# Stick-breaking attention: at most one scan piece between the transposes and the lower half, and y split one point after it is summed

## The chip, the core and the metric

The kernel runs on one core of a Trainium2 chip. The metric is the device time of one execution in microseconds. TensorE is written PE, VectorE DVE, ScalarE ACT, GpSimd POOL and SyncE, which only issues DMAs here, SP.

## What is computed

A decoder layer on 1024 positions of 1024 features in float32: half a SwiGLU feed-forward, two token mixers side by side (forgetting attention and stick-breaking attention, 8 heads of 64 each), a second half feed-forward, and a gated input embedding. The part that the change is in is the attention:

```python
def stick_breaking_attention(q, k, v):
    ...
        z = jnp.einsum('bqhd,bkhd->bhqk', qi, k).astype(jnp.float32) * scale
        mask = kpos[None, :] < pi[:, None]
        log_beta = jax.nn.log_sigmoid(z)
        log_1m = jnp.where(mask, jax.nn.log_sigmoid(-z), 0.0)
        after = lax.cumsum(log_1m, axis=3, reverse=True) - log_1m
        a = jnp.where(mask, jnp.exp(log_beta + after), 0.0)
        return jnp.einsum('bhqk,bkhd->bqhd', a.astype(v.dtype), v)
```

Forgetting attention is a causal softmax with an added bias; both end in the same product with v.

## The kernel before, in words

**Two halves.** A float32 factor is split into a higher half, rounded to the matmul's format, and a lower half, the rest. The higher half is a copy on ACT, the lower one a subtraction on DVE, and a product is the sum of two or three matmuls on these halves.

**Heads, steps and points.** `attention()` goes through 16 heads, of which the first 8 are forgetting attention ("fox") and the last 8 stick-breaking. A head has four steps c = 0 to 3. `scores` makes the two rows of 128 queries of a step (rows 2c and 2c+1): matmuls L1163 and L1164, then for stick-breaking the two sigmoids on ACT, G (L1171, buffers GF and RN in turn) and T (L1172). `apply` uses these rows two steps later. For each pair of key blocks (`kpair`, from c down to 0) `turn_and_scan` transposes the rows of T on PE into a bank of PSUM (L1222; there are two banks for it), copies the higher half out on ACT (L1224, tile PT), and subtracts the lower half out on DVE (`low`, L1230). `values` multiplies both halves with v (L1248) into the one bank `av`; the result is copied to the tile Y by ACT (L1274) and its other half added by DVE (L1277, `add`). In the first pair of a step the tile is 384 wide, in the others 512.

**Scans.** In stick-breaking the product over the later keys is a scan on DVE (L1126), in pieces of 256 keys of one row, and POOL then multiplies T by it (L1195). A piece is one scan, or two where it holds the diagonal (the masked 128 and the rest). Pieces wait in the list `pend`, and `pop()` takes one from it, or two when more than five wait; `pop(upto)` takes all up to a place in the order.

**Late work.** `late` holds what is done at the next `flush()`, of which there is one in each turn and one ahead of each row: the sum `add`, and behind it, when two heads and two steps of a Y tile are complete (`hh == 1 and c % 2`), y's division into halves: an ACT copy (L1283), a DVE subtraction (L1284) and two DMAs on SP (L1288, L1289) that write both halves to memory. The branch product reads them back (L1504) from head 13 on.

**Order.** PE's order in attention is the order of the code. For the last 8 heads ACT's copies L1224 and L1283 and DVE's instructions L1126, L1230, L1277 and L1284 keep the order of the code too (`order`); for the first 8 a list scheduler places them. In between, PE works on matmuls that fill up the time (L907, L915: projections of later heads; L1510: the branch product). POOL's L139 makes lower halves of weights from copies of ACT (L129).

Of the kernel before, what the change touches and what calls it, by code (L numbers as in the profile page):

```python
# [11 lines left out]
F32R = mybir.dt.float32r  # L12
# [6 lines left out]
P = 128  # L19
# [17 lines left out]
def tile_hybrid_decoder_layer(  # L37
# [6 lines left out]
    nc = tc.nc  # L44
# [7 lines left out]
    def nm(s):  # L52
        uid[0] += 1
        return f"{s}_{uid[0]}"

    def slot(tag, shape, dt=F32):
        pad = -shape[-1] % 16
        t = sb.tile([*shape[:-1], shape[-1] + pad], dt, tag=tag, bufs=BUFS[tag], name=nm(tag))
        return t[:, :, :shape[-1]] if pad else t
# [6 lines left out]
    def bank(tag):  # L66
        return pp.tile([P, 512], F32, tag=tag, bufs=PSUM[tag], name=nm("ps"))
# [12 lines left out]
    def pe(ins):  # L80
        order("pe", ins)

    def order(key, ins):
        prev = last.get(key)
        if prev is not None and not manual[0]:
            tc.add_manual_dep(ins.ins, prev.ins.name, NOSYNC, reason="order")
        last[key] = ins

    def f(ap):
        return ap.bitcast(F32)  # L90
# [72 lines left out]
    yd = dp.tile([8, 2, P, S], F32, name="y_pairs")  # L163
# [961 lines left out]
    def scan(*args):  # L1125
        order("dve", nc.vector.tensor_tensor_scan(*args))  # L1126

    def pop(upto=None):

        n = 1 + (len(pend) > 5)  # L1130
        while pend and (n if upto is None else pend[0][:2] <= upto):
            pend.pop(0)[2]()
            n -= 1

    pend, late = [], []

    def flush():
        while late:
            late.pop(0)()

    def scores(step, fill):
        step["pr"] = []
# [57 lines left out]
        for i in (2 * step["c"], 2 * step["c"] + 1):  # L1200
            pop((step["id"] - 2, 0))
            pop()
            flush()
            row(i)
            yield

    def apply(step, fill):
        c = step["c"]
        v2 = step["v"]["v"]
        hd = step["head"] % 4  # L1210
        av = bank("av")
        pts = {}

        def transposes(kpair):
            width = 512 if kpair < c else 384
            ps = bank("pt")
            for kb in (2 * kpair, 2 * kpair + 1):
                for j in range(2):
                    if kb == 2 * c + 1 and j == 0:
                        continue  # L1220
                    col = (kb % 2) * 256 + (j * P if kb < 2 * c + 1 else 0)
                    pe(nc.tensor.transpose(ps[:, col:col + P], step["pr"][j][:, kb * P:(kb + 1) * P], identf[:]))  # L1222
            pt = slot("PT", [P, 2, 512], F32R)
            high = nc.scalar.copy(pt[:, 0, :width], ps[:, :width])  # L1224
            if not step["fox"]:
                order("act", high)
            pts[kpair] = pt

            def low():
                ins = nc.vector.tensor_sub(pt[:, 1, :width], ps[:, :width], f(pt[:, 0, :width]))  # L1230
                if not step["fox"]:
                    order("dve", ins)
            return low

        def values(kpair):
            pt = pts[kpair]
            mm = []
            for kb in (2 * kpair, 2 * kpair + 1):
                for b in range(2):
                    c0 = (kb % 2) * 256  # L1240
                    if kb < 2 * c + 1:
                        mm.append((av[:, 0:256], v2[:, kb, hd, :], pt[:, b, c0:c0 + 256]))
                    else:
                        mm.append((av[:, P:256], v2[:, kb, hd, :], pt[:, b, c0:c0 + P]))
            if kpair == c:
                mm = [mm[0], mm[2], mm[3], mm[1]]
            for i, (o, lh, r) in enumerate(mm):
                pe(nc.tensor.matmul(o, lh, r, start=(kpair == c and i == 0), stop=(kpair == 0 and i == 3)))  # L1248

        def turn_and_scan(kpair):  # L1250
            low = transposes(kpair)
            pop()
            pop((step["id"], 2 - kpair))
            low()
            flush()
            fill()

        pop((step["id"], 1 - c))
        turn_and_scan(c)
        yield  # L1260
        for kpair in range(c - 1, -1, -1):
            turn_and_scan(kpair)
            if kpair + 2 <= c:
                values(kpair + 2)
            yield
        if c:
            values(1)
        fill()
        fill()
        values(0)  # L1270
        Y = step["y"]
        hh = step["head"] % 2
        ys = Y["t"][hh * HD:(hh + 1) * HD, c * 256:(c + 1) * 256]
        nc.scalar.copy(ys, av[HD:P, :256])  # L1274

        def add():
            ins = nc.vector.tensor_add(ys, av[0:HD, :256], ys)  # L1277
            if not step["fox"]:
                order("dve", ins)
            if hh == 1 and c % 2 and not step["last"]:  # L1280
                cs = slice(c // 2 * 512, c // 2 * 512 + 512)
                hi = slot("PT", [P, 512], F32R)
                a = nc.scalar.copy(hi[:], Y["t"][:, cs])  # L1283
                b = nc.vector.tensor_sub(Y["t"][:, cs].bitcast(F32R), Y["t"][:, cs], f(hi[:]))  # L1284
                if not step["fox"]:
                    order("act", a)
                    order("dve", b)
                nc.sync.dma_start(yd[Y["idx"], 0][:, cs], f(hi[:]))  # L1288
                nc.sync.dma_start(yd[Y["idx"], 1][:, cs], Y["t"][:, cs])  # L1289
        late.append(add)  # L1290

    FOX_PAIRS = [2, 3, 0, 1]
# [80 lines left out]
    def attention():  # L1373
# [109 lines left out]
        for step in prev:  # L1483
            run(apply(step, lambda: run(islice(rest, 6))))
        flush()
        run(rest)
        yt = ys[7]["t"]
# [340 lines left out]
```

## Time and profile before

| | |
|---|---|
| time, median of 3 runs | 2240.51 us (2239.74 to 2241.10) |
| the profiled execution: its own time, its span | 2238.65 us, 2236.9 us |
| PE busy | 2213.2 us, 99% of the span |
| DVE busy | 1515.7 us, 68% |
| ACT busy, POOL busy | 1004.8 us and 823.8 us |
| PE clock granted | 0.999 |
| transposes of attention, L1222 | from 849.9 us to 1372.1 us of the span |
| scans of stick-breaking, L1126 | from 1108.9 us to 1368.1 us |
| y's division, L1284 | 14 times, from 907.6 us to 1314.9 us |

In the rows a line stands for one group of instructions. In a timeline row the columns are start and duration in us, engine, line, operation, output and inputs, shapes and count; in brackets stands the idle time of the engine ahead of it and what ended that. In a row of waits stand who waited, for whom, the sum in us, how often, and the longest.

### The profile page before, as it was taken

Reading aid. Unit: us, or ns where it says so; the run is one execution under the profiler, and the core shown is the slowest. Engines: PE = TensorE matmul, PEld = TensorE weight load, DVE = VectorE, ACT = ScalarE, POOL = GpSimd, SP = SyncE. Lnnn points to the kernel's source line nnn. Section 1 sums busy time; section 2 is a strip of 40 time slices with the busy share of each in tenths; the row PEclk is TensorE's granted clock in tenths of the full one; section 3 lists DMA queues with packets and bytes.
Section 4 is the critical chain, followed back from the end, with each engine's and each line's share of the span. In section 5 each row is a group of like instructions: output and inputs, shape, how many; then the busy total and the mean of one; then the engine's idle time right before and its main releaser. Section 6 shows DMA issues by size and latency. Waiting matters only on the chain.

```text
span 2236.9 us, 30553 instructions
## 1 busy us (share of the span) xinstructions
PE 2213.2 (99%) x11226; PEld 1879.6 (84%) x11226; DVE 1515.7 (68%) x2365; ACT 1004.8 (45%) x1802; POOL 823.8 (37%) x793
## 2 busy tenths in 40 slices
PE   9999999999999999999999999999999999999998
PEld 7888888888888899999898888888888888888887
DVE  8855555598888324666678885789655455778897
ACT  6433333433455435555566663245333333333454
POOL 2444435200021336556556664520535344200111
PEclk9999999999999999999999999999999999999999
DMA  3332323394323334333324466741423232665336
GB/s 133 104 127 85 127 81 132 117 344 174 113 95 106 125 107 127 86 104 86 85 53 97 116 203 208 262 151 57 141 81 132 80 132 78 219 236 179 118 104 179
DMA packets 195607, 295.41 MB, mean 132 GB/s; under 512 B 28665, under 2 KB 108793, under 8 KB 195458
## 3 DMA queue, kind: packets, MB, share of 16 engines
q1 hardware_dynamic: 194448, 290.32, 39.2%
q0 software_dynamic: 1008, 3.15, 0.7%
q8 instruction: 88, 1.44, 0.3%
q14 instruction: 61, 0.50, 0.1%
q10 hardware_dynamic: 2, 0.00, 0.0%
HBM read 193.52 MB, written 83.13 MB: 124 GB/s over the span
## 4 chain that ended last, share of the span: by engine, by line
PE 88%; DVE 7%; ACT 2%; issue 1%; DMA 1%; POOL 0%; SPq 0%; DVEq 0%; ACTq 0%; POOLq 0%
PE ps L622 39%; PE ps L509 22%; PE ps L907 8%; PE ps L915 5%; PE ps L1510 4%; PE ps L1248 3%; PE ps L563 2%; PE ps L1222 2%; PE ps L1164 1%; PE ps L1163 1%; PE ps L1069 1%; DVE PT L1230 1%; DVE RN L1126 1%; DVE GF L1126 1%; DMA WH<-out_dram 1%
## 5 line engine op out<-in xcount | busy, mean ns | idle before, releaser
L509 PE MATMUL ps<-H,H 128*128 128x512 f32 x2184 | 497.3, 389 | 0.0
L509 PEld LDWEIGHTS ps<-H,H 128*128 128x128 f32 x2184 | 409.5, 188 | 84.9
L622 PE MATMUL ps<-H,WL 128*128 128x512 f32 x1164 | 275.0, 389 | 0.0
L622 PEld LDWEIGHTS ps<-H,WL 128*128 128x128 f32 x1164 | 218.5, 188 | 45.3
L185 POOL TENSOR_TENSOR PT<-PT,PT 128x512 f32<-128x512 f32 x27 | 34.9, 1294 | 403.8 <-ACT PT L182 402.9
L622 PE MATMUL ps<-H,Q 128*128 128x512 f32 x612 | 145.5, 389 | 0.0
L517 DVE SCALAR_TENSOR_TENSOR X<-ps,X 128x512 f32<-128x512 f32 x168 | 110.0, 683 | 47.5 <-PE ps L509 47.3
L622 PE MATMUL ps<-X,WL 128*128 128x512 f32 (+1 forms) x588 | 139.1, 386 | 2.6 <-ACT KH L1789 2.6
L622 PEld LDWEIGHTS ps<-H,Q 128*128 128x128 f32 x612 | 114.9, 188 | 23.8
L622 PE MATMUL ps<-H,PT 128*128 128x512 f32 x540 | 129.1, 390 | 1.6 <-ACT PT L105 0.9
L622 PEld LDWEIGHTS ps<-X,WL 128*128 128x128 f32 x588 | 109.2, 188 | 24.9 <-ACT KH L1789 2.8
L139 POOL TENSOR_TENSOR WL<-RAW,WH 128x512 fp32r<-128x512 f32 (+1 forms) x84 | 98.4, 1193 | 67.5 <-ACT WH L129 43.2
L622 PEld LDWEIGHTS ps<-H,PT 128*128 128x128 f32 x540 | 101.1, 188 | 23.4 <-ACT PT L105 1.3
L1230 DVE TENSOR_TENSOR PT<-ps,PT 128x512 fp32r<-128x512 f32 (+1 forms) x160 | 99.8, 626 | 29.6 <-ACT PT L1224 28.9
L907 PE MATMUL ps<-WH,H 128*128 128x256 f32 x768 | 116.1, 287 | 0.8 <-ACT RN L972 0.8
L915 PE MATMUL ps<-H,WH 128*128 128x512 f32 x384 | 115.0, 406 | 0.0
L1248 PE MATMUL ps<-PT,X 128*128 128x256 f32 (+1 forms) x640 | 102.3, 286 | 6.4 <-DVE PT L1230 5.4
L1224 ACT CAST PT<-ps 128x512 fp32r<-128x512 f32 (+1 forms) x160 | 87.1, 548 | 42.6 <-PE ps L1222 41.5
L1248 PEld LDWEIGHTS ps<-PT,X 128*128 128x128 f32 x640 | 90.2, 190 | 16.7 <-DVE PT L1230 10.2
L907 PEld LDWEIGHTS ps<-WH,H 128*128 128x128 f32 x768 | 101.4, 190 | 2.6 <-ACT RN L972 1.2
L412 POOL TENSOR_TENSOR PT<-GF,RN 128x512 f32<-128x512 f32 x20 | 33.6, 1682 | 185.3 <-DVE GF L815 185.3
L1176 POOL TENSOR_TENSOR T<-T,l 128x128 f32<-128x128 f32 (+3 forms) x64 | 73.2, 1147 | 71.8 <-DVE l L1175 69.7
(457 smaller groups left out, 4793.2 us busy)
## 6 DMA issues: line engine op xcount, KB each, us to landing
hidden<-PT SPq DMA_DIRECT2D x40, 512.0 KB, 3.1
WH<-in_ffn_w_gate_dram SPq DMA_DIRECT2D x38, 512.0 KB, 5.5
Q<-hidden SPq DMA_DIRECT2D x24, 512.0 KB, 5.6
hidden<-RN SPq DMA_DIRECT2D x22, 512.0 KB, 2.6
KH<-in_ffn_w_up_dram SPq DMA_DIRECT2D x20, 512.0 KB, 6.2
KL<-in_ffn_w_up_dram SPq DMA_DIRECT2D x20, 512.0 KB, 6.9
T<-in_ffn_w_down_dram SPq DMA_DIRECT2D x20, 512.0 KB, 6.2
GF<-hidden SPq DMA_DIRECT2D x14, 512.0 KB, 6.9
```

What stands on the lines that cost most here:

```text
L139: ins = eng_lo.tensor_sub(lo[part], raw[part], f(hi[part]))
L509: pe(nc.tensor.matmul(groups[g][t][:], wt[:, b, k, t * P:(t + 1) * P], act[:, a, k, :], start=(fresh and n == 0), stop=(i in (6, 1, 4) and ...
L517: nc.vector.scalar_tensor_tensor(xs, groups[g][t][:], scale, xs, ALU.mult, ALU.add)
L563: pe(nc.tensor.matmul(ps[:], hl[:, a, k, :], right(rb, b, k), start=(i == 0), stop=(i == 23)))
L622: pe(nc.tensor.matmul(ps[:, cols], hl[:, a, k, :], right(B[m], b, k)[:, cols], start=(first and i == 0), stop=(final and i == 11), skip_gr ...
L907: pe(nc.tensor.matmul(ps[:, :n], hT[t // 4](a, k)[:, (t % 4) * P:(t % 4 + 1) * P], w[k // 4][b][:, k % 4, :n], start=(i == 0), stop=(i == ...
L915: pe(nc.tensor.matmul(ps[:], w[a][:, k, :], hT[half](b, k), start=(i == 0), stop=(i == 23)))
L1176: nc.gpsimd.tensor_mul(T[:, :n], T[:, :n], l[:].broadcast_to([P, n]))
L1224: high = nc.scalar.copy(pt[:, 0, :width], ps[:, :width])
L1230: ins = nc.vector.tensor_sub(pt[:, 1, :width], ps[:, :width], f(pt[:, 0, :width]))
L1248: pe(nc.tensor.matmul(o, lh, r, start=(kpair == c and i == 0), stop=(kpair == 0 and i == 3)))
L1510: pe(nc.tensor.matmul(ps[:], w[a][:, k, :], yT[g][b][:, k, half * 512:half * 512 + 512], start=(i == 0), stop=(i == 11)))
```

## The change

`turn_and_scan` takes one piece from `pend` between the transposes and `low`; the second piece, if more than five were waiting, and the pieces that `pop(upto)` asks for come behind `low`. `flush` calls only what was in `late` when it began, and `add` no longer divides y itself but puts that into `late`, so that it comes at the next point.

```diff
-    def pop(upto=None):
+    def pop(upto=None, n=None):
 
-        n = 1 + (len(pend) > 5)
+        n = n or 1 + (len(pend) > 5)
...
     def flush():
-        while late:
-            late.pop(0)()
+        for call in [late.pop(0) for _ in range(len(late))]:
+            call()
...
         def turn_and_scan(kpair):
             low = transposes(kpair)
-            pop()
+            more = len(pend) > 5
+            pop(n=1)
+            low()
+            if more:
+                pop(n=1)
             pop((step["id"], 2 - kpair))
-            low()
             flush()
             fill()
...
             if hh == 1 and c % 2 and not step["last"]:
-                cs = slice(c // 2 * 512, c // 2 * 512 + 512)
-                hi = slot("PT", [P, 512], F32R)
-                a = nc.scalar.copy(hi[:], Y["t"][:, cs])
-                b = nc.vector.tensor_sub(Y["t"][:, cs].bitcast(F32R), Y["t"][:, cs], f(hi[:]))
...
+                late.append(parts)
+
+        def parts():
+
+            cs = slice(c // 2 * 512, c // 2 * 512 + 512)
+            hi = slot("PT", [P, 512], F32R)
+            a = nc.scalar.copy(hi[:], Y["t"][:, cs])
+            b = nc.vector.tensor_sub(Y["t"][:, cs].bitcast(F32R), Y["t"][:, cs], f(hi[:]))
...
```

PE's order is the same in both kernels. In the changed kernel's lines L1277 stands at L1280, L1283 at L1290 and L1284 at L1291. A scan has the name SCALAR_TENSOR_TENSOR in the lists of the order and TENSOR_TENSOR_SCAN in the trace.

The first place is DVE's order where two heads of the first half of attention end, at 981 us of the trace: L1284 divides y, L1230 are lower halves, L1168 and L1175 belong to the softmax. Before:

```order
L993 SCALAR_TENSOR_TENSOR KL_9214<-ps_9215,gqk,KH_9213 128x512
L1284 TENSOR_TENSOR Y_8277<-Y_8277,PT_9196 128x512
L1175 RECIPROCAL l_9203<-l_9203 128x1
L1230 TENSOR_TENSOR PT_9231<-ps_9227,PT_9231 128x384
L1168 ISA T_9234,m_9235<-T_9234,ps_9238,m_9235 128x128
L1168 ISA m_9235 128x1
L1230 TENSOR_TENSOR PT_9255<-ps_9250,PT_9255 128x512
```

And now:

```order
L993 SCALAR_TENSOR_TENSOR KL_9209<-ps_9210,gqk,KH_9208 128x512
L1175 RECIPROCAL l_9198<-l_9198 128x1
L1230 TENSOR_TENSOR PT_9226<-ps_9222,PT_9226 128x384
L1291 TENSOR_TENSOR Y_8277<-Y_8277,PT_9229 128x512
L1168 ISA T_9234,m_9235<-T_9234,ps_9238,m_9235 128x128
L1168 ISA m_9235 128x1
L1230 TENSOR_TENSOR PT_9255<-ps_9250,PT_9255 128x512
```

The division of y has moved from ahead of the 384-wide lower half to behind it; on ACT its copy has moved behind the higher half of the same tile.

The second place is DVE's order in a stick-breaking head, at 1259 us of the trace, where more than five pieces wait: L1126 are scans, L1230 lower halves. Before:

```order
L1126 SCALAR_TENSOR_TENSOR RN_11786<-RN_11786 128x256
L1126 SCALAR_TENSOR_TENSOR GF_11754<-GF_11754 128x255
L1230 TENSOR_TENSOR PT_11847<-ps_11843,PT_11847 128x384
L1126 SCALAR_TENSOR_TENSOR RN_11786<-RN_11786 128x255
L1126 SCALAR_TENSOR_TENSOR GF_11827<-GF_11827,mask_sb 128x128
L1126 SCALAR_TENSOR_TENSOR RN_11861<-RN_11861,mask_sb 128x128
L1126 SCALAR_TENSOR_TENSOR RN_11861<-RN_11861 128x128
L1230 TENSOR_TENSOR PT_11881<-ps_11876,PT_11881 128x512
L1126 SCALAR_TENSOR_TENSOR GF_11827<-GF_11827 128x256
```

And now:

```order
L1126 SCALAR_TENSOR_TENSOR RN_11786<-RN_11786 128x256
L1230 TENSOR_TENSOR PT_11847<-ps_11843,PT_11847 128x384
L1126 SCALAR_TENSOR_TENSOR GF_11749<-GF_11749 128x255
L1126 SCALAR_TENSOR_TENSOR RN_11786<-RN_11786 128x255
L1126 SCALAR_TENSOR_TENSOR GF_11827<-GF_11827,mask_sb 128x128
L1230 TENSOR_TENSOR PT_11881<-ps_11876,PT_11881 128x512
L1126 SCALAR_TENSOR_TENSOR RN_11861<-RN_11861,mask_sb 128x128
L1126 SCALAR_TENSOR_TENSOR RN_11861<-RN_11861 128x128
L1126 SCALAR_TENSOR_TENSOR GF_11827<-GF_11827 128x256
```

Each of the two lower halves has moved ahead of one piece: the 384-wide one ahead of a single scan, the 512-wide one ahead of the two scans of a diagonal piece. This pattern stands once in each of the eight stick-breaking heads, and in the last one a further lower half moves ahead of a scan; the other lower halves have as many scans ahead of them as before.

More of the change, by code (lines that the diff above doesn't have):

```diff
@@ L1280, in add @@
             if hh == 1 and c % 2 and not step["last"]:
-                cs = slice(c // 2 * 512, c // 2 * 512 + 512)
-                hi = slot("PT", [P, 512], F32R)
[L1283 to L1289, printed above, removed]
+                late.append(parts)
[4 more added lines that the diff above has]
+            b = nc.vector.tensor_sub(Y["t"][:, cs].bitcast(F32R), Y["t"][:, cs], f(hi[:]))
+            if not step["fox"]:
+                order("act", a)
+                order("dve", b)
+            nc.sync.dma_start(yd[Y["idx"], 0][:, cs], f(hi[:]))
+            nc.sync.dma_start(yd[Y["idx"], 1][:, cs], Y["t"][:, cs])
         late.append(add)
```

## Prediction

> **What bounds the kernel now.** I read the page first: which engine is busy. Then the list of PE's waits, cut to attention (840 to 1380 us), since PE's order does not change and only a wait of PE can change in length; then the timelines around the single waits.
>
> ```profile
> PE 2213.2 (99%) x11226; PEld 1879.6 (84%) x11226; DVE 1515.7 (68%) x2365; ACT 1004.8 (45%) x1802; POOL 823.8 (37%) x793
> ```
>
> PE is idle for 2236.9 - 2213.2 = 23.7 us in all. An edit that leaves PE's work alone can win no more than its part of that, and it loses what it adds to it. The two longest rows of who waited for whom in attention, with sum, times and longest:
>
> ```profile
> PE ps L1248 <- DVE PT L1230: 5.4, 12, 1.3
> PE ps L1222 <- DVE PT L1230: 4.3, 6, 1.2
> ```
>
> Both are waits for a lower half, L1230, 5.4 + 4.3 = 9.7 us: the product with v (L1248) waits for the data, the transposes (L1222) wait for the bank that the lower half still reads. So the edit is aimed at the right instruction, and the question is which of these 18 waits it touches. No row of that list names POOL: the products behind the scans are early enough now.
>
> **Part one: y's division moves behind the lower half.** The rows of DVE's subtraction and of its idle time:
>
> ```profile
> L1284 DVE TENSOR_TENSOR Y<-Y,PT x14: 681/700/1544, 907.6 to 1314.9; 128x512 fp32r<-128x512 f32 x14
>   ACT PT L1283: 5.1, 7
> ```
>
> It takes at least 0.68 us, and seven of the fourteen wait for ACT's copy, 5.1 us together, at the head of DVE's queue. The order shows where it stood right ahead of a 384-wide lower half. Five waits of transposes lie just behind such a place, or one scan further:
>
> ```profile
> 908.84 0.66 PE L1222 MATMUL ps<-identf,T 128*128 128x128 f32 x4 [0.28 <-DVE PT L1230]
> 983.33 0.63 PE L1222 MATMUL ps<-identf,T 128*128 128x128 f32 x4 [1.18 <-DVE PT L1230]
> 1047.79 0.63 PE L1222 MATMUL ps<-identf,T 128*128 128x128 f32 x4 [0.64 <-DVE PT L1230]
> 1111.60 0.65 PE L1222 MATMUL ps<-identf,T 128*128 128x128 f32 x4 [0.88 <-DVE PT L1230]
> 1174.98 0.63 PE L1222 MATMUL ps<-identf,T 128*128 128x128 f32 x4 [0.44 <-DVE PT L1230]
> ```
>
> Three of them (0.28, 0.64 and 0.44 us) are shorter than the 0.68 us that leave the queue ahead of the lower half, and go, if ACT's higher half is there: that is the next thing to be late. The place at 983 us shows that it is.
>
> ```profile
> 980.59 0.61 ACT L1283 CAST PT<-Y 128x512 fp32r<-128x512 f32 x1
> 981.49 0.95 ACT L1224 CAST PT<-ps 128x384 fp32r<-128x384 f32 x2
> 981.58 1.07 DVE L1284 TENSOR_TENSOR Y<-Y,PT 128x512 fp32r<-128x512 f32 x1
> 982.65 0.53 DVE L1230 TENSOR_TENSOR PT<-ps,PT 128x384 fp32r<-128x384 f32 x1
> ```
>
> The higher half starts at 981.49, behind y's copy. Without that copy it can be done by about 981.5, and DVE, free at 981.58, puts only the reciprocal first: the lower half starts near 981.72 instead of 982.65, and 0.93 of the 1.18 us goes. At 1111.60 the lower half stood behind the division:
>
> ```profile
> 1110.36 0.71 DVE L1284 TENSOR_TENSOR Y<-Y,PT 128x512 fp32r<-128x512 f32 x1
> 1110.99 0.55 DVE L1230 TENSOR_TENSOR PT<-ps,PT 128x384 fp32r<-128x384 f32 x1
> ```
>
> It moves from 1110.99 to 1110.36, which takes 0.63 off the 0.88 us. Sum of part one: 0.28 + 0.93 + 0.64 + 0.63 + 0.44 = 2.92 us.
>
> What moves along is ACT's copy, past one higher half, and two DMAs on SP, past one load of weights or some copies of q and k. Nobody waits for them soon: what they write is first read from head 13 on, and a write lands in some us:
>
> ```profile
> DMA to landing us min/median/max: 2.0/2.8/5.8
> ```
>
> That is the row of L1288. The PT buffer that holds y's higher half is taken one turn later and given back one turn later; I price this at nothing, and if a copy had to wait for its landing, it would cost PE up to those 2.8 us at one place. In the fox heads the scheduler also swaps a few of DVE's, ACT's and POOL's instructions that PE does not wait for in the list above; zero, with 0.5 us either way.
>
> **Part two: the second piece moves behind the lower half.** Here is the place of the second list, once per stick-breaking head, at 1259 us. DVE first, then ACT's higher halves.
>
> ```profile
> 1259.35 0.71 DVE L1126 TENSOR_TENSOR_SCAN GF<-GF 128x255 f32<-128x255 f32 x1
> 1260.67 0.56 DVE L1230 TENSOR_TENSOR PT<-ps,PT 128x384 fp32r<-128x384 f32 x1 [0.60 <-ACT PT L1224]
> ...
> 1261.83 0.39 DVE L1126 TENSOR_TENSOR_SCAN GF<-GF,mask_sb 128x128 f32<-128x128 f32 x1
> 1262.15 0.79 DVE L1126 TENSOR_TENSOR_SCAN RN<-RN,mask_sb 128x128 f32<-128x128 f32 x1
> 1262.97 0.48 DVE L1126 TENSOR_TENSOR_SCAN RN<-RN 128x128 f32<-128x128 f32 x1
> 1263.81 0.69 DVE L1230 TENSOR_TENSOR PT<-ps,PT 128x512 fp32r<-128x512 f32 x1 [0.35 <-ACT PT L1224]
> ...
> 1265.08 0.73 DVE L1126 TENSOR_TENSOR_SCAN RN<-RN 128x256 f32<-128x256 f32 x1
> 1265.91 0.69 DVE L990 TENSOR_TENSOR KL<-ps,KH 128x512 fp32r<-128x512 f32 x1
> ...
> 1270.78 0.66 DVE L1230 TENSOR_TENSOR PT<-ps,PT 128x512 fp32r<-128x512 f32 x1
> ```
>
> ```profile
> 1260.13 0.51 ACT L1224 CAST PT<-ps 128x384 fp32r<-128x384 f32 x1
> 1263.16 0.62 ACT L1224 CAST PT<-ps 128x512 fp32r<-128x512 f32 x1
> ```
>
> Both lower halves already wait for ACT, 0.60 and 0.35 us: the scans ahead of them run while DVE has nothing better to do. The higher halves end at 1260.64 and 1263.78 whatever DVE does, so neither lower half can start earlier. What changes is that DVE now stands idle ahead of them, and the scans come after. The diagonal pair, which ran from 1262.15 to 1263.45, has to fit in behind 1263.81, and all that follows is later by up to its 1.30 us (0.9, if its first scan takes 0.39 like its neighbour instead of 0.79). Only idle time takes that off again: here 1265.91 - (1265.08 + 0.73) = 0.10 us. About 1.1 us arrive at the lower half of 1270.78, and there PE is already waiting:
>
> ```profile
> 1271.49 0.62 PE L1248 MATMUL ps<-PT,X 128*128 128x256 f32 x3 [0.27 <-DVE PT L1230]
> ```
>
> This costs 1.1 us. The same pattern comes 62 us later with the same wait for ACT, and again without slack, since the lower half ends at 1332.34 and the product with it had started at 1331.76:
>
> ```profile
> 1322.42 0.56 DVE L1230 TENSOR_TENSOR PT<-ps,PT 128x384 fp32r<-128x384 f32 x1 [0.60 <-ACT PT L1224]
> 1331.68 0.66 DVE L1230 TENSOR_TENSOR PT<-ps,PT 128x512 fp32r<-128x512 f32 x1
> 1331.76 1.26 PE L1248 MATMUL ps<-PT,X 128*128 128x256 f32 x8
> ```
>
> Another 1.1 us. In the head at 1200 us DVE idles afterwards,
>
> ```profile
> 1204.10 0.69 DVE L990 TENSOR_TENSOR KL<-ps,KH 128x512 fp32r<-128x512 f32 x1 [0.80 <-ACT KH L989]
> ```
>
> which swallows 0.8 us; of the 0.3 to 0.4 us left I take 0.2. In the heads at 1165, 1230 and 1292 us the division of y stood a little behind the pattern, and the time that it no longer waits for ACT (5.1 us / 7 = 0.7 us) and its own 0.68 us come out of the same queue ahead of the next lower half; I take zero there, and for the first head, at 1132 us, too. In the last head it is the other way round: the 512-wide lower half stood behind a slow diagonal pair, and PE waited.
>
> ```profile
> 1355.93 0.62 PE L1248 MATMUL ps<-PT,X 128*128 128x256 f32 x3 [0.31 <-DVE PT L1230]
> ```
>
> These 0.31 us go, since the pair is longer than that. Sum of part two: 1.1 + 1.1 + 0.2 - 0.31 = +2.1 us.
>
> Later scans mean later products on POOL and later transposes two steps on. PE waits for none of them today; 1.3 us more is about one turn, and I price it at zero.
>
> **The sum.** -2.92 + 2.1 = -0.8 us against the execution's own 2238.65 us: 2237.8 us. The median of the runs is 1.86 us above that execution, so 2240.51 - 0.8 = **2239.7 us**. A measurement of this kernel can tell about 0.2%, 4.5 us, from no change; my forecast is no change, and its own range, with the two losses of 1.1 us at 0 or doubled, is 2237.5 to 2242 us.
>
> **The rivals.**
>
> *The late pair reaches PE in every head.* It is 1.1 us in each of seven heads if nothing swallows it: 7.7 - 2.92 - 0.31 = +4.5 us, 2245.0 us. For it speaks that DVE is busy without a gap from 1266 to 1271 us; against it the 0.8 us of idle time at 1204 us and the division that leaves the queue. It decides at the second lower half behind the pattern, where PE has no slack or some tenths. Chance 0.17.
>
> *The scans are held up by POOL.* A scan of 255 or 256 keys takes 740 ns in the median, but not always, while lower halves hardly vary:
>
> ```profile
> L1126 DVE TENSOR_TENSOR_SCAN GF<-GF x48: 715/740/1704, 1116.9 to 1363.4; 128x255 f32<-128x255 f32 x24, 128x256 f32<-128x256 f32 x24
> L1230 DVE TENSOR_TENSOR PT<-ps,PT x160: 524/658/693, 851.1 to 1374.0; 128x512 fp32r<-128x512 f32 x96, 128x384 fp32r<-128x384 f32 x64
> 1266.80 3.51 POOL L139 TENSOR_TENSOR WL<-RAW,WH 128x512 fp32r<-128x512 f32 x2
> ```
>
> The moved scans may fall under the long POOL instructions for the weights, which were running then. If the three heads without cover each meet one more, it costs 3 x (1.704 - 0.740) = 2.9 us: 2239.7 + 2.9 = 2242.6 us. They may leave such a meeting as well. Chance 0.14. The Trainium skill says why, under "SBUF — State Buffer", section "Who interferes with whom": a DVE instruction with two inputs in SBUF and a GpSimd instruction that reads SBUF exclude each other for the whole instruction. Scan and lower half differ just so (the lower half reads one input from PSUM), and the two rows above agree.
>
> *The scans cost nothing.* If the diagonal pair runs at its short times and the next lower halves have room, only the gains are left, with the 0.27 us at 1271: -2.92 - 0.31 - 0.27 = -3.5 us, 2237.0 us; with half of the 5.4 us that products wait for lower halves as well, 2234.3 us. Against it: the two waits for ACT of 0.60 and 0.35 us. Chance 0.23.
>
> *Nothing reaches PE.* The waits only change places, 2240.5 us; chance 0.06. It would need the five waits of transposes to stay. My forecast has 0.40.
>
> **The numbers.** The range goes from the low end of the third rival to just past the first, 2234.3 to 2246 us. Faster by over 0.2% (below 2236.0): 0.13, half of the third rival and a little of the forecast's tail. Slower by over 0.2% (above 2245.0): 0.14, the upper half of the first rival and the two first together. Within: 0.73.
>
> **What would show it.** In the changed kernel's trace the waits of L1222 for L1230 fall from 4.3 us to about 1.4, and none of the five stays above 0.3 us. DVE's waits of L1230 for ACT's L1224 grow, by some 1 us in each stick-breaking head. L1248's waits for L1230 grow by about 2 us, at the places that were 1271 and 1332 us. I am wrong if the waits of the transposes stay (ACT's higher half was the limit), if L1248's waits grow in all heads, or if PE begins to wait for POOL.

## The result, and the profile after

The changed kernel takes 2244.36 us (median; 2242.61 to 2246.11), the kernel before, run beside it, 2240.86 us (2239.07 to 2242.05): a ratio of 1.0016, 95% interval 1.0009 to 1.0022. That is 3.5 us more. It lies inside the range (2234.3 to 2246.0) and below the 0.2% that I called no change, but it is surely slower, and the forecast was 0.8 us faster.

The page's row of busy times of the kernel after:

```profile
PE 2216.5 (99%) x11226; PEld 1880.2 (84%) x11226; DVE 1521.0 (68%) x2365; ACT 1005.4 (45%) x1802; POOL 824.7 (37%) x793
```

Its list of PE's waits in attention, 840 to 1385 us (sum, times, longest):

```profile
PE ps L1248 <- DVE PT L1230: 10.5, 18, 1.3
PE ps L1248 <- ACT PT L1224: 1.6, 3, 1.1
PE ps L1222 <- DVE PT L1230: 1.4, 3, 0.9
```

And of DVE's waits, 1100 to 1385 us:

```profile
DVE PT L1230 <- ACT PT L1224: 26.0, 25, 5.3
```

The transposes (L1222) wait 1.4 us instead of 4.3: this gain came as forecast. The products with v (L1248) wait 10.5 us for lower halves instead of 5.4, and 1.6 instead of 0.5 for higher halves. DVE stands 11 us longer at the head of its queue for ACT's higher halves (14.9 before).

PE's order is the same in both kernels, so each of its instructions can be set beside its counterpart, and where the difference of the two start times steps, time was lost or won. These steps are the most exact view of such a change. In attention they add up to +4.2 us; another 2.3 us of the two profiled executions' difference arises in the first 19 us of the span, where the kernels do the same; set against the kernel before, the traces of this case differ by 0.2 to 2.4 us ahead of attention, so this part is not put down to the change. The gains, at the times of before: -0.44 (908.84), -0.98 (983.33), -0.60 (1047.79), -0.64 (1111.60), -0.60 (1174.98) and -0.47 us (1355.93), in sum -3.73. The losses: +0.68 (1113.13), +1.26 (1176.93), +0.71 (1209.25), +0.50 (1239.82), +0.96 (1271.49), +0.50 (1302.18), +0.80 (1332.40) and +1.85 us (1374.1), in sum +7.26; what is missing to +4.2 are steps below 0.25 us. PE's timeline of the kernel after shows them as waits:

```profile
1113.44 0.62 PE L1248 MATMUL ps<-PT,X 128*128 128x256 f32 x3 [0.52 <-DVE PT L1230]
...
1177.98 0.62 PE L1248 MATMUL ps<-PT,X 128*128 128x256 f32 x3 [1.17 <-DVE PT L1230]
...
1211.01 0.61 PE L1248 MATMUL ps<-PT,X 128*128 128x256 f32 x3 [0.55 <-DVE PT L1230]
...
1242.17 0.51 PE L1248 MATMUL ps<-PT,X 128*128 128x256 f32 x2 [0.59 <-DVE PT L1230]
...
1275.09 0.62 PE L1248 MATMUL ps<-PT,X 128*128 128x256 f32 x3 [1.23 <-DVE PT L1230]
...
1306.30 0.39 PE L1248 MATMUL ps<-PT,X 128*128 128x256 f32 x1 [0.60 <-DVE PT L1230]
...
1337.47 0.63 PE L1248 MATMUL ps<-PT,X 128*128 128x256 f32 x3 [0.70 <-DVE PT L1230]
...
1379.77 0.39 PE L1248 MATMUL ps<-PT,X 128*128 128x256 f32 x1 [1.07 <-ACT PT L1224]
1380.50 0.61 PE L1248 MATMUL ps<-PT,X 128*128 128x256 f32 x3 [0.34 <-DVE PT L1230]
```

From the second to the seventh stick-breaking head there is one such wait (1177.98 to 1337.47). It is not at the next lower half behind the moved diagonal pair, which is 384 wide, but at the 512-wide one behind that, a turn later. The last head waits at its end, at 1379.77. Scans are not only late there but long. POOL and DVE of the kernel after in the head at 1200 us:

```profile
1206.52 3.32 POOL L139 TENSOR_TENSOR WL<-RAW,WH 128x512 fp32r<-128x512 f32 x2
...
1207.03 0.53 DVE L1230 TENSOR_TENSOR PT<-ps,PT 128x384 fp32r<-128x384 f32 x1
1207.48 1.27 DVE L1126 TENSOR_TENSOR_SCAN RN<-RN 128x256 f32<-128x256 f32 x1
1208.67 1.71 DVE L1126 TENSOR_TENSOR_SCAN GF<-GF 128x255 f32<-128x255 f32 x1
1210.30 0.66 DVE L1230 TENSOR_TENSOR PT<-ps,PT 128x512 fp32r<-128x512 f32 x1
```

And the same place in the kernel before:

```profile
1204.29 2.92 POOL L139 TENSOR_TENSOR WL<-RAW,WH 128x512 fp32r<-128x512 f32 x2
...
1206.05 0.53 DVE L1230 TENSOR_TENSOR PT<-ps,PT 128x384 fp32r<-128x384 f32 x1
1206.50 1.25 DVE L1126 TENSOR_TENSOR_SCAN RN<-RN 128x256 f32<-128x256 f32 x1
1207.68 0.72 DVE L1126 TENSOR_TENSOR_SCAN GF<-GF 128x255 f32<-128x255 f32 x1
```

None of these instructions of DVE has changed its place; the pair that moved ran ahead of them, at 1202.97 and 1203.42. PE is 1.05 us later here than before, and by that clock the 384-wide lower half is on time again (1206.05 + 1.05 = 1207.10). What came later is POOL: its halves of the weights (1206.52 to 1209.84) start 2.23 us later, 1.2 us more than PE, because POOL's products wait for the late pair (1.19 us, at 1204.05). So they now meet the second scan too, which takes 1.71 us instead of 0.72, while the lower half keeps its 0.53.

### The profile page after: what moved, and what is told of

Read it like the earlier page. It is cut to its first block, busy times and chain, and to the rows that moved or that the text cites. A ratio compares the mean times of both kernels' runs of the same rounds, so it can differ in the third digit from the quotient of the medians.

```text
span 2242.9 us, 30553 instructions
## 1 busy us (share of the span) xinstructions
PE 2216.5 (99%) x11226; PEld 1880.2 (84%) x11226; DVE 1521.0 (68%) x2365; ACT 1005.4 (45%) x1802; POOL 824.7 (37%) x793
## 5 line engine op out<-in xcount | busy, mean ns | idle before, releaser
L1230 DVE TENSOR_TENSOR PT<-ps,PT 128x512 fp32r<-128x512 f32 (+1 forms) x160 | 99.8, 627 | 40.0 <-ACT PT L1224 39.2
L1248 PE MATMUL ps<-PT,X 128*128 128x256 f32 (+1 forms) x640 | 103.2, 286 | 12.4 <-DVE PT L1230 10.5
L1248 PEld LDWEIGHTS ps<-PT,X 128*128 128x128 f32 x640 | 90.5, 190 | 23.5 <-DVE PT L1230 15.9
L412 POOL TENSOR_TENSOR PT<-GF,RN 128x512 f32<-128x512 f32 x20 | 33.7, 1686 | 185.0 <-DVE GF L815 185.0
```

## The experiments

All were timed beside the kernel before, in three sessions in which that took 2240.68, 2241.05 and 2240.61 us.

**Each part alone.** The first kernel is the changed one without the edit in `turn_and_scan`; the second is the changed one without `parts`, y being divided in `add` as before, and with the old `flush`.

```diff
             low = transposes(kpair)
-            more = len(pend) > 5
-            pop(n=1)
-            low()
-            if more:
-                pop(n=1)
+            pop()
             pop((step["id"], 2 - kpair))
+            low()
```

```diff
             if hh == 1 and c % 2 and not step["last"]:
-                late.append(parts)
+                cs = slice(c // 2 * 512, c // 2 * 512 + 512)
...
```

> Part one alone: y's division comes one point later, the scans keep their old places. Theory A (part one wins, the late pieces of part two lose): the five waits of the transposes go as in the changed kernel (0.44, 0.98, 0.60, 0.64 and 0.60 us by the steps between the two traces), the new wait at 1113 us (0.68 us) stays, the rest as before: -2.6 us against before, about 2238.3 us. Rival B (the losses in the heads at 1177, 1240 and 1302 us come from the division, which now stands between the two lower halves): those 2.3 us stay too, and the kernel is within 0.5 us of before.

> Part two alone: the second piece behind the lower half, y divided in place as before. Theory A: the losses of the changed kernel without its gains, +0.7, +1.0, +0.8 and the 1.9 us at 1374 us, less 0.5 us, and in the three heads where y is divided 0.5 us or more each: +5 to +7 us, 2246 to 2248 us. Rival B: without the division between the lower halves the three heads lose nothing: +4 us, 2245 us.

Part one alone: 2237.83 us (2236.01 to 2239.30), ratio 0.9987 [0.9979, 0.9996], -2.85 us. Part two alone: 2247.29 us (2245.36 to 2248.75), ratio 1.0030 [1.0019, 1.0041], +6.6 us. Together +3.8 us, against 3.5 measured: the parts add up within the noise, and the net loss is in part two; part one has a loss of its own, 0.68 us at 1113 us. PE's waits in attention with part one alone:

```profile
PE ps L1248 <- DVE PT L1230: 5.8, 13, 1.2
PE ps L1222 <- DVE PT L1230: 1.3, 3, 0.9
```

**Where part two loses: the last head, the diagonal pair.** In the first of these the last head has its old order of scans; in the second the diagonal pair stays ahead of the lower half, and only single scans move.

```diff
             pop(n=1)
+            if more and step["id"] >= 60:
+                pop(n=1)
             low()
-            if more:
+            if more and step["id"] < 60:
                 pop(n=1)
```

```diff
             pop(n=1)
+            diagonal = more and len(pend) and -pend[0][1] == pend[0][0] % 4
+            if diagonal:
+                pop(n=1)
             low()
-            if more:
+            if more and not diagonal:
                 pop(n=1)
```

> The changed kernel with the old scan order in the last head alone. Theory A says that the 1.9 us at 1374 us come from the late scans of this head, through POOL and a load of gates behind them on SP: they go, and the 0.5 us gain at 1356 us goes with them: 1.4 us below the changed kernel, 2243.0 us. Rival (the load is late because the whole head starts later, by the losses of the heads before): no change against the changed kernel, 2244.4 us, or 0.5 us above.

> The changed kernel, but the second piece moves behind the lower half only where it is a single scan; the two scans of a diagonal piece stay ahead of the 512-wide lower half. Theory A (what costs is DVE's idle time ahead of lower halves that wait for ACT): the single scan is 0.65 us, of which the old idle time of 0.35 us at the 512-wide lower half takes up half, so the delay behind the pattern is 0.3 us instead of 1.3: five of the six losses in the heads go nearly, and the kernel is at before - 1.5 to -2.5 us plus what is left at 1374 us, 2238.5 to 2240.5 us. Rival (it is not the idle time but where the scans meet POOL): no clear relation, losses of 2 us and more stay, over 2242 us.

The old last head: 2243.66 us (2242.62 to 2245.81), ratio 1.0014 [1.0006, 1.0023], 0.7 us less than the changed kernel instead of 1.4; its step at 1374 us falls from 1.85 to 0.42, and the -0.47 of 1355.93 goes with it. The diagonal pair ahead: 2241.45 us (2240.49 to 2243.46), ratio 1.0003 [0.9994, 1.0012]. The steps at 1240 and 1302 go, that at 1332 shrinks to 0.24, and 0.47 at 1266 stand in place of 0.96 at 1271; those at 1177 (0.73) and 1209 (0.42) stay in part, and the last head loses 1.10 at 1355.93. So moving the pair makes 2.9 us of the loss, not all of it. The time is 1 us above what theory A expected and below the 2242 us of its rival, so it decides for neither. Single scans that move cost something too.

**What POOL has to do with it.** In the first pair of kernels POOL fills the lower halves of the weights with zeros instead of subtracting: it writes the same tiles and reads nothing there; its products (L1195) go on reading. The orders on PE, DVE and ACT are those of the kernels without the fill; only POOL's and some of SP's differ.

```diff
-            ins = eng_lo.tensor_sub(lo[part], raw[part], f(hi[part]))
+            ins = eng_lo.memset(f(lo[part]), 0.0) if filling[0] else eng_lo.tensor_sub(lo[part], raw[part], f(hi[part]))
```

> The kernel before, but from head 8 on POOL's lower halves of the weights (L139) are replaced by a fill with zeros, so that POOL only writes there and reads nothing; the lower halves of these weights are lost from the output. It serves as the base for its counterpart with both parts of the change. Both theories: scans stay at 0.7 to 0.8 us where POOL ran the weights' halves, 2236 to 2241 us.

> The changed kernel with the same fill in place of POOL's lower halves of the weights from head 8 on. Theory A (about half of what the later scans cost comes from POOL: scans that were stretched to 1.1 to 1.8 us by the weights' halves, and the weights' halves that in turn gave their buffers back later and so held up SP's loads at the end): the difference to the unchanged kernel with the fill falls from +3.5 to between 0 and +1.5 us, with the steps at 1209 and 1374 us below 0.3 us. Rival B (DVE stands idle at the head of its queue and the scans are late by their own plain length): the difference stays at +2.5 us or more, and the steps at 1177, 1209, 1240 and 1374 us stay as they are.

Before with fill: 2237.91 us (2236.68 to 2239.12), ratio 0.9988 [0.9979, 0.9996]. After with fill: 2237.28 us (2235.18 to 2238.59), ratio 0.9983 [0.9974, 0.9992]. With the fill the change brings -0.6 us instead of +3.5, a little below the 0 to +1.5 of theory A. The fill makes the changed kernel faster by 7.1 us, and the kernel before by only 3.1 us. The steps of 1177, 1209, 1271 and 1332 are below 0.3 us; 0.49 us each stay at 1240 and 1302, and 0.74 at 1373, where theory A had less than 0.3; the fill does not reach that place, as shown below. The gains shrink as well: in the kernel before with fill, the waits at 1111.60 and 1174.98 are gone (steps of -0.93 and -0.60 us against the kernel before), though DVE's order is the same.

But a fill is also shorter (0.53 us against 1.3 to 1.5 us), so that POOL's queue is free earlier. The second pair does each fill three times.

```diff
+            if filling[0]:
+                for _ in range(2):
+                    order("wl", eng_lo.memset(f(lo[part]), 0.0))
```

> The kernel before with the fill, but each fill is done three times, so that POOL is busy about as long as with the weights' halves (3 x 0.53 = 1.6 us against 1.47 us for 512 elements, 3 x 0.31 = 0.93 against 0.86 us for 256) and still reads nothing; the lower halves of the weights are lost as before. Base for its counterpart. If it is POOL's reading that stretches scans, the time stays at that of the single fill, 2237 to 2239 us; if POOL's busy time matters, it goes back towards 2241 us.

> The changed kernel with the triple fill. Theory A (scans are stretched because POOL reads): the time stays near that of the single fill, 2236.5 to 2238.5 us, the difference to its counterpart is between -1 and +1 us, and the steps at 1177 and 1209 us stay below 0.3 us. Rival B (POOL's queue is late because its instructions take long, whatever they read): POOL's products come later again, the time rises by 2 us or more over the single fill, and the steps at 1177 and 1209 us come back with some 0.7 us or more each.

Before: 2236.12 us (2235.02 to 2239.14), ratio 0.9982 [0.9973, 0.9991]; after: 2238.15 us (2236.01 to 2238.85), ratio 0.9988 [0.9979, 0.9997]. The times do not go back up by what the weights' halves had cost: the changed kernel stays 6.2 us below its own time without fill. The kernel before is 0.9 us faster than the 2237 to 2239 I expected. The difference of the two medians, 2.0 us, misses my -1 to +1; by the spread of the eleven runs of each it lies between about 0.3 and 2.9 us (95%), so the change still costs something here, but whether more than 1 us the runs do not decide. The steps say less: +0.7 us in attention in all, nothing above 0.3 at 1177 and 1209, about 0.5 each at 1240, 1279 and 1301, and 1.18 at 1372, against -0.47 at 1354 and the gains of part one. Rows of DVE's scans GF (min/median/max in ns), of the kernel after:

```profile
L1126 DVE TENSOR_TENSOR_SCAN GF<-GF x48: 715/741/1775, 1117.4 to 1368.3; 128x255 f32<-128x255 f32 x24, 128x256 f32<-128x256 f32 x24
```

After with fill:

```profile
L1128 DVE TENSOR_TENSOR_SCAN GF<-GF x48: 714/740/1312, 1114.3 to 1359.4; 128x255 f32<-128x255 f32 x24, 128x256 f32<-128x256 f32 x24
```

After with triple fill, the scans, and POOL's two extra fills of 512 (us in sum, mean ns, 1100 to 1385 us):

```profile
L1131 DVE TENSOR_TENSOR_SCAN GF<-GF x48: 711/738/1312, 1114.6 to 1359.8; 128x255 f32<-128x255 f32 x24, 128x256 f32<-128x256 f32 x24
```

```profile
L143 POOL MEMSET WL<- 128x512 f32 x36 | 18.9, 524 | 0.7
```

All 192 scans together (the sum of the nine groups of their line) take 134 us before and 137 us after, 127 and 128 with the fill, 126 and 126 with the triple fill, although POOL is busy with these fills for longer than with the subtractions that they stand for (28 times three fills take 39.0 us in the changed kernel, the 28 subtractions 33.7 us). In the head at 1165 us, where the division takes 1.26 us and the last scan ahead of the lower half 1.06 us in the kernel after, DVE and POOL with the triple fill:

```profile
1170.65 0.68 DVE L1296 TENSOR_TENSOR Y<-Y,PT 128x512 fp32r<-128x512 f32 x1
1171.25 0.74 DVE L1131 TENSOR_TENSOR_SCAN RN<-RN 128x256 f32<-128x256 f32 x1
1171.91 0.72 DVE L1131 TENSOR_TENSOR_SCAN GF<-GF 128x255 f32<-128x255 f32 x1
...
1170.60 0.53 POOL L144 MEMSET WL<- 128x512 f32 x1
1171.07 0.53 POOL L143 MEMSET WL<- 128x512 f32 x1
```

POOL is busy beside all three, and none is stretched. For the scans it is the reading, then, not the time that POOL works. The Trainium skill says in "SBUF — State Buffer", section "Who interferes with whom", that a DVE instruction with two inputs in SBUF contends with a GpSimd instruction that reads SBUF, and not with one that only writes it; the runs agree, with 1.71 us for a scan beside POOL's subtraction and 0.72 us beside its fill.

The fills leave one meeting as it is, that with POOL's products, which read too. Behind the late pair two of them fall on the scan that follows. In the head at 1165 us, before, after, and after with triple fill:

```profile
1168.88 0.73 DVE L1126 TENSOR_TENSOR_SCAN RN<-RN 128x256 f32<-128x256 f32 x1
```

```profile
1169.72 0.93 POOL L1195 TENSOR_TENSOR T<-T,RN 128x255 f32<-128x255 f32 x1 [1.23 <-DVE RN L1126]
1170.61 1.02 POOL L1195 TENSOR_TENSOR T<-T,GF 128x256 f32<-128x256 f32 x1
...
1170.13 1.06 DVE L1126 TENSOR_TENSOR_SCAN RN<-RN 128x256 f32<-128x256 f32 x1
```

```profile
1167.41 1.06 DVE L1131 TENSOR_TENSOR_SCAN RN<-RN 128x256 f32<-128x256 f32 x1
```

This scan takes 1.06 us in seven of the eight heads in every kernel where the pair is late in them, with fill or without, and 0.72 to 0.73 us in those heads where the pair is ahead. That the products stretch it is read from these rows; no run takes the products away.

**The end of attention.** The step of 1.85 us at 1374 us is another mechanism. POOL, SP, ACT and DVE of the kernel after:

```profile
1366.61 0.64 POOL L1195 TENSOR_TENSOR T<-T,RN 128x256 f32<-128x256 f32 x1 [0.69 <-DVE RN L1126]
1367.21 1.88 POOL L139 TENSOR_TENSOR WL<-RAW,WH 128x256 fp32r<-128x256 f32 x2
...
1369.11 0.38 SPq L119 DMA_DIRECT2D RAW<-in_w_branch_fox_dram  x1
1369.59 0.93 SPq L1657 DMA_DIRECT2D T<-gates  x2
1370.57 0.42 SPq L1657 DMA_DIRECT2D KL<-gates  x1
...
1378.19 1.06 ACT L1659 ACTIVATE KL<-KL 128x1024 f32<-128x1024 f32 x1 [4.77 <-DMA KL<-gates]
1379.15 1.05 ACT L1224 CAST PT<-ps 128x512 fp32r<-128x512 f32 x2
...
1379.75 0.69 DVE L1230 TENSOR_TENSOR PT<-ps,PT 128x512 fp32r<-128x512 f32 x1 [5.26 <-ACT PT L1224]
```

Late scans make POOL's products late, and these make the weights' lower half late; SP's load of the next weight (L119) waits for that buffer, a gate's load (L1657) stands behind it on SP, ACT waits 4.77 us for the gate, and a higher half of attention stands behind ACT's sigmoid. Before, the load on SP went out at 1362.83: 6.3 us earlier, where PE stood 4.5 us earlier. One edit cuts this chain and moves little else:

```diff
-        nc.sync.dma_start(gs[m][:], gd[KD + m].rearrange("p (h n) -> p h n", h=2))
+        (nc.scalar if m == 4 else nc.sync).dma_start(gs[m][:], gd[KD + m].rearrange("p (h n) -> p h n", h=2))
```

> The changed kernel, but the load of the fifth gate (tile KL, L1657) is issued by ACT, early, instead of standing on SP behind the load of a weight that waits for POOL. Theory A (the 1.85 us lost at 1374 us come down the chain late scans, POOL's weight halves, SP's queue, the gate, ACT's sigmoid, the higher half behind it): at least 1.2 of the 1.85 us go, 2242.5 to 2243.2 us. Rival B (the lower halves at 1374 us are late because DVE's own scans are late): the step stays at 1.5 us or more and the time is within 0.4 us of the changed kernel's, 2244.4 us.

2242.31 us (2241.16 to 2243.67), ratio 1.0006 [0.9997, 1.0014], 2.05 us below the changed kernel. The step is gone whole (-1.24 and -0.61), while all others stand to 0.01 us as they were. The list of waits shows what is left of L1248's waits for ACT, 1.6 us before this edit:

```profile
PE ps L1248 <- ACT PT L1224: 0.6, 2, 0.3
```

The fills say nothing of this chain, since they are switched off behind the last head: from 1348 us on POOL subtracts in those kernels too, beside a scan of 1.31 us, and ACT waits for this gate again, 3.93 and 5.11 us in the changed kernel with the single and the triple fill.

**The loss at 1113 us.** It comes with part one alone too, so it is not of the scans. The edit puts y's division three points later instead of one.

```diff
-                late.append(parts)
+                late.append(lambda: late.append(lambda: late.append(parts)))
```

> The first part of the change alone, but with y's division three points later instead of one, so that it stands behind the next 512-wide lower half too. If the 0.68 us lost at 1113 us with the first part come from the division ahead of that lower half, the step at 1113 us goes and the time is 0.5 to 1 us below that of the first part alone, 2236.8 to 2237.4 us. If the division only moves the loss on to the next lower half, the time is that of the first part, 2237.8 us, and a new step stands one turn on.

2237.05 us (2235.68 to 2238.81), ratio 0.9984 [0.9975, 0.9993]. DVE with part one alone:

```profile
1109.62 0.76 DVE L1288 TENSOR_TENSOR Y<-Y,PT 128x512 fp32r<-128x512 f32 x1
...
1111.24 1.26 DVE L1230 TENSOR_TENSOR PT<-ps,PT 128x512 fp32r<-128x512 f32 x2
```

And with the division three points later:

```profile
1111.48 0.67 DVE L1230 TENSOR_TENSOR PT<-ps,PT 128x512 fp32r<-128x512 f32 x1
1112.06 0.83 DVE L1288 TENSOR_TENSOR Y<-Y,PT 128x512 fp32r<-128x512 f32 x1
```

The row of 1111.24 holds two lower halves, of which the first is the late one. PE runs 0.94 us later at this place in the second trace, so against PE this lower half starts 0.70 us earlier there. PE's step of 0.68 us between the two is the only one over 0.25 us, and nothing new stands one turn on. The medians differ by 0.8 us, which by itself these runs cannot tell from nothing; against the kernel before, both are faster beyond their intervals, and the later division has the lowest median of the kernels that leave nothing out: 4.0 us below the kernel before, 7.3 below the changed one.

## Why the prediction was wrong, point by point

- **Part one, -2.92 us: right, its total by some luck.** Alone it measured -2.85 us. The five waits went or shrank as priced; no step is over 0.16 us from its term. What I did not see is that the division, one place later, stands right ahead of the next lower half, 512 wide: +0.68 us at 1113 us, where that lower half had ended 0.15 us ahead of its product. The five steps are 0.34 us more than priced, and 0.21 and 0.26 us at 1239.82 and 1302.18 that I had not counted offset the rest. Two of the five waits were also made by POOL: at 1111.60 behind a scan of 1.51 us, at 1174.98 behind a division of 1.48 us, both beside POOL's halves of the weights; with the fill they go without the edit.
- **Part two, +2.1 us: mis-sized, and this is the step that failed.** Alone it measured +6.6 us. Nearly all of the 4.5 us between is in three terms, by the steps of the whole change: zero for the heads with division (2.26 us), zero for POOL's later products (1.85 us), and 0.2 for 0.71 us. The two losses priced at 1.1 us each (1271 and 1332) came as 0.96 and 0.80, and the last head's gain as -0.47 for -0.31. That the two sizes are so near is partly luck: at 1271 the three scans around the 384-wide lower half took 0.73, 1.23 and 1.70 us before and 1.40, 1.85 and 0.72 us after, and without POOL's reading of weights both places keep less than 0.3 us.
- **"I take zero there": wrong.** The three heads with division lost 1.26, 0.50 and 0.50 us. I let the division pay for the pair twice, with its wait for ACT and with its own length. The wait is gone, and the 384-wide lower half is on time. But the division's length has only moved: it stands between the two lower halves now, ahead of the 512-wide one, where PE waits. The kernel after in the head at 1230 us:

```profile
1238.86 0.53 DVE L1230 TENSOR_TENSOR PT<-ps,PT 128x384 fp32r<-128x384 f32 x1
1239.31 0.90 DVE L1291 TENSOR_TENSOR Y<-Y,PT 128x512 fp32r<-128x512 f32 x1
...
1241.46 0.66 DVE L1230 TENSOR_TENSOR PT<-ps,PT 128x512 fp32r<-128x512 f32 x1
```

The division by itself costs nothing there: part one alone has no such loss. Part two alone loses 0.92, 0.50 and 0.49 us in these heads, at the transposes ahead (1174.98, 1238.09 and 1300.45): the pair reaches PE there with the division in either place. At 1177 POOL's halves of the weights add to it, beside a scan of 1.77 us and a division of 1.26 us.
- **"I take 0.2" at 1209 us: 0.71.** The idle time took up the pair's delay more fully than I said, since the 384-wide lower half is on time again; the loss is a scan that did not move and takes 1.71 us under POOL's weights, which came later.
- **Zero for POOL's later products: wrong by 1.85 us.** PE does not wait for POOL in the changed kernel either; the delay came round through SP's queue, a DMA and ACT, where my list of what a late scan holds up ended at the transposes.
- **The rivals.** The first said that the pair reaches PE in every head: it did in six, with 0.5 to 1.26 us each (4.73 us in sum, against 7.7 forecast), and its 2245.0 us is the nearest to the 2244.36 measured. That is partly luck, since the end of attention, 1.85 us, was not in it. The second was scans held up by POOL. The fills show that most of the loss needs POOL's reading of the weights: without it the change is worth -0.6 and +2.0 us in the two pairs, by the steps -0.2 and +0.7, and the losing steps ahead of the end of attention sum to 1.6 and 2.0 us instead of 5.4. I had given it a chance of 0.14 and the three heads without cover; it also struck heads that I had called covered.
- **What stays open.** How the 0.5 us that remain at 1240 and 1302 with the fills are shared between the plain lateness of the pair and the 0.34 us that the scan behind it takes longer beside POOL's products; whether +2.0 or +0.7 us is the truth for the triple fill; and how much of the fills' effect is fewer meetings of scans with POOL, and how much the room that DVE gains everywhere when no scan is stretched. The scans' sum grows by 3.2 us from before to after, and by 1.7 and -0.1 us with the fills. That is 1.5 to 3.3 us of scan time, while the steps' sum in attention is 4.4 and 3.5 us smaller, so both may have a part; nothing tells the two apart in each head.

## What to carry to other kernels

Work that stands ahead of an instruction that already waits is free there; moved behind it, it keeps its full length and pushes everything that follows, so it has to be priced at each later place without idle time, with credit only for work that really leaves the queue ahead of that place. Before moving VectorE work with two SBUF inputs, look at what GpSimd reads at the new time as well as at the old one. And follow a late instruction through the buffers that it frees: here one turn's delay came back to PE by way of a DMA queue and ScalarE.

## What the runs showed of the hardware

I had not expected how much of the kernel's time hangs on this meeting of DVE and POOL. In the kernel before, where no wait of PE in attention names POOL, letting POOL write the weights' halves without reading gains 3.1 us with the single and 4.5 us with the triple fill, though the halves are lost from the output; and not scans alone are stretched: y's division, which has two inputs in SBUF too, takes 1.48 us before and 1.26 us after at 1172 and 1174 us, against 0.68 us with the triple fill, while a lower half, with one input in PSUM, keeps its 0.53 us beside the same instruction of POOL. The stretch goes the other way as well: POOL's two weight halves at 1206.52 take 3.32 us, where twice the line's median of 1.29 us is 2.58 us; the difference, 0.74 us, is about one scan.
